# Hybrid decoder block in float32: raw weight blocks in two rings, block sums in a tile of their own, and later squares in the output units

## The chip, the cores and the metric

The kernel runs on one core of one Trainium2 chip. The metric is the device time of one execution in microseconds (us). Before the change three executions took 2388.03, 2392.00 and 2387.68 us, median 2388.03 us; lower is better. A run of this kernel can be told from "no change" at about 0.2%.

## The reference, cut to what matters

One sequence of 256 tokens and 4096 channels in float32 goes through one block. Everything that costs time is matrix products of the 256 x 4096 activations with large weights that are read once:

```
h     = rmsnorm(x, norm_w)
proj  = h @ w_in                     # 4096 x 20480, split in u_p z_p u_c b_c c_c z_c and two gate logits
y_pool = pool(u_p) @ pool_w * pool_scale * silu(z_p)      # four windows 2, 4, 8, 16
y_conv = b_c * conv3(c_c * u_c) * silu(z_c)
merged = sigmoid(g0) * (y_pool @ w_branch[0]) + sigmoid(g1) * (y_conv @ w_branch[1])
out    = rmsnorm(x + merged @ w_out, final_norm_w)
```

`w_in` is 335 MB, `w_branch` 67 MB, `w_out` 67 MB. The results have float32 accuracy.

## The kernel before, in words

**Products.** A float32 number is written as a high part, rounded to the type that TensorE reads fast (`fp32r`), and a low part, the difference. A product is three matmuls: high x high, high x low, low x high. The work is cut into units of 1024 output columns (20 of `w_in`, 8 of `w_branch`, 4 of `w_out`), and a unit into steps (16, or 8 for `w_branch`). A step takes 256 input channels x 1024 columns of weights: four blocks of 128 x 512, in the host's order q0 to q3, 2 KB per partition each. There are two kinds of step. A plain step "P" multiplies the four blocks directly: 8 products, 24 matmuls of 128 x 128 by 128 x 512. A step "S" is one level of a Strassen-like scheme: 7 products, 21 matmuls. It needs the blocks q0, q1, q2 as they are, the corner w = q3 + q2 (the addition is made by an accumulating DMA), and three sums: w - q1, q0 - (w - q1) and q2 - (w - q1). The activations' side of either kind stands ready in SBUF. A unit's order of steps is a text, such as `TEN = "PSPSSPSSPSSPSSPS"` for the gate units or `NINE = "PSPSPSPSSPSPSSPS"` for the second and third output unit. In the last S of a unit ("closing") the order of the seven products is another one. An S runs M2 (block q0), N3 (q1), M1 (q2), N5 (w), N6, N7, N4 (the sums), a closing one M2, N3, N4, M1, N7, N5, N6, three matmuls each. The units in order, with their texts (B and M are small steps of the pooling branch):

```
cz0 16 x P | cb0 NINE_A | cu0 NINE | cc0 NINE_A | cz1 SIX5 | cb1 TEN | cu1 NINE | cc1 NINE_A
pz0 SIX5 | pu0 NINE_P | pz1 HOST | pu1 NINE_P | g0_0 HOST | six gate units TEN | g1_0 SEVEN3
b0_0 B0 | b1_0 B1_FIRST | then three times: b0 B0_MORE, b1 B1 | o0 SIX5 | o1 NINE | o2 NINE | o3 OUT3
SIX5 PPPPPSPSPSPSPSPS   SEVEN3 PPPSPSPSPSPSPSPS   NINE PSPSPSPSSPSPSSPS   NINE_A PSPSSPSPSSPSPSPS
NINE_P PSPSSPSPSSPSSPSP   TEN PSPSSPSSPSSPSSPS   HOST PPBPPMMPSSPSSPSSPSS   OUT3 PSPSPSPSPSPSSPPP
B0 PPPPSPSP   B0_MORE PPPPSSPS   B1_FIRST PPSPSPSP   B1 PSPSPSPP
```

**Preparing a step.** SyncE's queue loads the blocks into a raw slot (`load`, L77): one transfer of 1 MB for P; for S one of 256 KB for q3, one of 768 KB for q0 to q2, and then GpSimd's queue issues the accumulating transfer of q2 onto q3 (`gather`, L89). There are NRAW = 5 raw slots of 8 KB per partition; a slot is loaded again when the step in it is wholly prepared (`prepared`). ScalarE writes the high parts (`highs`, L59) and VectorE the low parts and the sums (`lows` and `sub`, L62). They go to a ring of 26 cells of 2 KB. Cells are given out in order round the ring; a group of cells can be taken when the products that read their former contents have been written into TensorE's program, and on the chip when these have run. A P takes 4 + 4 cells. An S takes 3 + 3 + 4 + 4 cells: high parts of q0 to q2, their low parts, then high and low parts of two blocks twice (`outer`: w - q1 and w; `inner`: the other two sums). The sums overwrite the raw slot.

**Order.** All engines run one hand-written order. While TensorE's matmuls of a step are written down, `pump` writes as much of the preparation of the following steps as the ring and the raw slots allow. Each engine runs its own instructions strictly in that order. Work at the end of a unit (its epilogue) is a list in `queue`: after every 6 matmuls (a tick) one entry is taken off; `gap(n)` is n empty entries. `combine` and `corner_sums` add the unit's separate sums (tile `J`) at the unit's end.

**Output units.** After the output unit c < 3 the epilogue adds the J sums into `E` with two accumulating transfers on GpSimd's queue, adds the rows of x into E with two more (`row`), loads the norm weights with ScalarE's queue (`start`), squares and sums the rows of E on ScalarE (`square`), multiplies E by the weights on VectorE and stores E to `o_d`. The last unit loads these back into raw slots (`unpark`), and the rest of x into another one (`rest`).

Of the kernel before, what the change touches and what calls it, by code (L numbers as in the profile page):

```python
# [27 lines left out]
NRAW = 5  # L28
# [23 lines left out]
def hybrid_block(ctx: ExitStack, tc: tile.TileContext, x, xc, prm, rows_in, w_in, pool_w, w_branch, w_out, out):  # L52
# [56 lines left out]
    raw = sb("raw", [P, NRAW, 2 * NU])  # L109
# [145 lines left out]
    class Step:  # L255
        def __init__(self, unit, kind, src=None, op=None, **kw):
            self.unit, self.kind, self.src, self.op = unit, kind, src, op
            self.__dict__.update(kw)
            self.raw = None
            self.prepared = self.halved = False  # L260
            self.pre, self.mid = [], []

        def first(self):
# [3 lines left out]
            def rounded(cells):  # L267
                self.q = self.raw.rearrange("p (i c) -> p i c", i=4)
                self.cells = cells
                if self in steps[:2]:  # L270
                    for i in range(4):
                        if self is steps[0] and i == 0:
                            copy(ring[:, cells[0]], self.q[:, 0])
                        else:
                            highs(cells[i:i + 1], self.q[:, i:i + 1])
                elif self.halved:
                    for i in (0, 2):
                        highs(cells[i:i + 2], self.q[:, i:i + 2])
                else:
                    highs(cells, self.q[:, 0:len(cells)])  # L280

            return [(3 if self.kind == "S" else 4, None, rounded)]

        def rest(self):
            if self.kind == "P":
                def rests(to):
                    self.lows = to
                    if self in steps[:2]:
                        for i in range(4):
                            if self is steps[0] and i % 2 == 0:  # L290
                                x_low(0, 1 - i // 2)
                            lows(to[i:i + 1], self.cells[i:i + 1], self.q[:, i:i + 1])
                    elif self.halved:
                        for i in (0, 2):
                            lows(to[i:i + 2], self.cells[i:i + 2], self.q[:, i:i + 2])
                    else:
                        lows(to, self.cells, self.q)

                return [(4, None, rests)] + self.mid
            if self.kind == "S":  # L300
                def whole(to):
                    self.lows = to
                    c, q = self.cells, self.q
                    lows(to[1:2], c[1:2], q[:, 1:2])
                    lows([to[0], to[2]], [c[0], c[2]], q[:, 0:3:2])

                def outer(cells):
                    q = self.q
                    self.outer = cells
# [966 lines left out]
```

## Time and profile before

| what | value |
|---|---|
| three executions | 2387.68, 2388.03, 2392.00 us |
| the profiled execution's own time | 2385.66 us |
| its span, first to last instruction | 2383.9 us (1.8 us lie around it) |
| TensorE busy | 2346.6 us, 98% of the span, 10424 matmuls and transposes |
| VectorE busy | 2138.2 us, 90% |
| ScalarE busy | 1488.3 us, 62% |
| GpSimd busy | 287.0 us, 12% |
| mean granted TensorE clock | 0.995 |
| DMA | 627.7 MB, 263 GB/s mean |

PE is TensorE's matmuls, PEld its weight loads, DVE is VectorE, ACT is ScalarE, POOL is GpSimd, SP is SyncE; a name with q (SPq, POOLq) is the engine's queue of DMA issues. "raw<-in_w_in_dram" is a load of input weights into the raw tile. A timeline row starts with the start and the length in us; "x3" means three like instructions merged; in brackets stands how long the engine was idle before it and what ended that. Because matmuls overlap, the row's length holds the drain of the last one.

### The profile page before, as it was taken

The numbers are of one execution on the slowest core, as the hardware profiler recorded it, in microseconds if no ns is written. First come the engines' busy times: TensorE is split into PE (matmuls) and PEld (weight loads), VectorE is DVE, ScalarE is ACT, GpSimd is POOL, SyncE is SP. The second block draws the span as 40 slices with busy tenths as digits, with TensorE's granted clock in tenths as the row PEclk, the third lists the DMA queues.
The fourth block names the chain that finished last, engine by engine and source line by source line (L and its number), as shares of the span: only waits on it lengthen the run. The fifth ranks groups of instructions, "written<-read, shape, count | busy, mean of one in ns | idle before, by whom it ended". The sixth has DMA issues, their size and how long they took to land.

```text
span 2383.9 us, 28821 instructions
## 1 busy us (share of the span) xinstructions
PE 2346.6 (98%) x10424; PEld 1938.5 (81%) x10424; DVE 2138.2 (90%) x2208; ACT 1488.3 (62%) x1565; POOL 287.0 (12%) x342
## 2 busy tenths in 40 slices
PE   9999999999999999999999999999999999999997
PEld 7888888888888888888888888888878887887785
DVE  8799988999979979979999999988998888998887
ACT  6665655756656656656766666665756656556564
POOL 0001100111001201201111111110000100011110
PEclk9999999999999999999999999999999999999998
DMA  9789876988868768868999999999978888887996
GB/s 385 242 254 282 251 239 213 282 258 252 262 221 247 265 197 253 262 199 253 283 284 282 284 303 285 283 281 298 272 226 282 252 281 281 255 256 237 288 271 230
DMA packets 167711, 627.70 MB, mean 263 GB/s; under 512 B 17424, under 2 KB 25872, under 8 KB 135568
## 3 DMA queue, kind: packets, MB, share of 16 engines
q1 hardware_dynamic: 101792, 485.40, 56.9%
q0 software_dynamic: 48128, 98.59, 23.3%
q10 hardware_dynamic: 17648, 41.87, 5.0%
q8 instruction: 81, 1.33, 0.2%
q14 instruction: 62, 0.51, 0.1%
HBM read 579.66 MB, written 25.17 MB: 254 GB/s over the span
## 4 chain that ended last, share of the span: by engine, by line
PE 89%; DMA 4%; DVE 3%; issue 2%; ACT 1%; POOL 0%; SPq 0%; DVEq 0%; ACTq 0%; POOLq 0%
PE sums L1054 64%; PE shared L1054 23%; DVE ring L62 2%; DMA raw<-in_w_out_dram 1%; PE shared L696 1%; DMA E<-in_x_dram 1%; DMA raw<-in_w_branch_dram 1%; PE shared L482 1%; ACT ring L59 1%; DMA E<-J 1%; DMA raw<-in_w_in_dram 1%; DMA raw<-in_x_dram 0%; DVE E L62 0%; DVE raw L62 0%; POOL E L89 0%
## 5 line engine op out<-in xcount | busy, mean ns | idle before, releaser
L59 ACT ACTIVATE ring<-raw 128x1024 fp32r<-128x1024 f32 (+3 forms) x1089 | 1226.1, 1171 | 748.5 <-DVE raw L62 555.2
L1054 PE MATMUL sums<-ring,arena 128*128 128x512 f32 x7011 | 1642.5, 390 | 13.5 <-DVE ring L62 11.1
L62 DVE TENSOR_TENSOR ring<-raw,ring 128x1024 fp32r<-128x1024 f32 (+2 forms) x1338 | 1467.2, 1141 | 147.8 <-ACT ring L59 73.8
L1054 PEld LDWEIGHTS sums<-ring,arena 128*128 128x128 f32 x7011 | 1313.5, 188 | 290.4 <-DVE ring L62 15.5
L1054 PE MATMUL shared<-ring,arena 128*128 128x512 f32 x2241 | 545.8, 391 | 7.6 <-ACT ring L59 5.5
L1054 PEld LDWEIGHTS shared<-ring,arena 128*128 128x128 f32 x2241 | 422.3, 189 | 98.0 <-ACT ring L59 6.3
L62 DVE TENSOR_TENSOR raw<-raw 128x512 f32<-128x512 f32 (+1 forms) x444 | 424.4, 956 | 10.0 <-DMA raw<-in_w_out_dram 2.3
L89 POOL DMA_DIRECT2D raw<-in_w_in_dram x168 | 145.5, 866 | 1362.9 <-DMA raw<-in_w_in_dram 572.1
L62 DVE TENSOR_TENSOR J<-J 128x512 f32<-128x512 f32 (+1 forms) x90 | 78.2, 869 | 14.7 <-ACT J L59 12.5
L1054 PE MATMUL sums<-ring,last_pair 128*128 128x512 f32 x306 | 76.2, 389 | 0.0
L59 ACT ACTIVATE J<-shared 128x512 f32<-128x512 f32 x128 | 69.9, 601 | 4.2 <-PE shared L482 2.9
L1054 PEld LDWEIGHTS sums<-ring,last_pair 128*128 128x128 f32 x306 | 57.4, 188 | 11.9
L59 ACT ACTIVATE E<-sums 128x512 f32<-128x512 f32 x76 | 41.8, 598 | 28.4 <-PE sums L1054 27.6
L89 POOL DMA_DIRECT2D raw<-in_w_out_dram x31 | 28.0, 904 | 258.5 <-DMA raw<-in_w_out_dram 85.5
L89 POOL DMA_DIRECT2D raw<-in_w_branch_dram x23 | 20.0, 869 | 302.4 <-DMA raw<-in_w_branch_dram 142.2
L1054 PE MATMUL shared<-ring,last_pair 128*128 128x512 f32 x216 | 51.9, 389 | 0.0
L1054 PE MATMUL shared<-ring,side 128*128 128x512 f32 x207 | 50.7, 389 | 0.0
L1054 PEld LDWEIGHTS shared<-ring,last_pair 128*128 128x128 f32 x216 | 40.6, 188 | 8.4
L1054 PEld LDWEIGHTS shared<-ring,side 128*128 128x128 f32 x207 | 38.9, 188 | 8.1
L89 POOL DMA_DIRECT2D E<-J x28 | 38.9, 1469 | 13.4 <-ACT ring L59 13.4
L62 DVE TENSOR_TENSOR E<-E,Y 128x2048 f32<-128x2048 f32 x9 | 20.6, 2287 | 7.2 <-ACT Y L59 7.1
L59 ACT ACTIVATE E<-E 128x1024 f32<-128x1024 f32 x16 | 16.7, 1048 | 11.6 <-DMA E<-in_x_dram 11.6
(120 smaller groups left out, 594.7 us busy)
## 6 DMA issues: line engine op xcount, KB each, us to landing
raw<-in_w_in_dram SPq DMA_DIRECT2D x150, 1024.0 KB, 7.2
raw<-in_w_in_dram SPq DMA_DIRECT2D x168, 768.0 KB, 6.8
raw<-in_w_in_dram SPq DMA_DIRECT2D x176, 256.0 KB, 5.1
raw<-in_w_in_dram POOLq DMA_DIRECT2D x168, 256.0 KB, 6.7
raw<-in_w_branch_dram SPq DMA_DIRECT2D x41, 1024.0 KB, 7.5
raw<-in_w_out_dram SPq DMA_DIRECT2D x33, 1024.0 KB, 6.9
raw<-in_w_out_dram SPq DMA_DIRECT2D x31, 768.0 KB, 7.1
raw<-in_w_branch_dram SPq DMA_DIRECT2D x23, 768.0 KB, 6.9
```

What stands on the lines that cost most here:

```text
L59: return pin(nc.scalar.activation(dst, src, func, **kw))
L62: return pin(nc.vector.tensor_tensor(out=dst, in0=a, in1=b, op=op))
L89: return pin(nc.gpsimd.dma_start(dst, src, accum_op=ALU.add))
L482: pin(nc.tensor.transpose(shared(j)[:, i * T + t * P:i * T + (t + 1) * P], src[:, t, c:c + P], ident))
L696: pin(nc.tensor.matmul(o, a, b, start=(k, i) == (0, 0), stop=(k, i) == (3, 2)))
L1054: pin(nc.tensor.matmul(ps, lhs, rhs, start=n == 0, stop=n == u.total[b] - 1))
```

## The change

The raw tile becomes two rings: four places of 6 KB per partition for q0 to q2, and five places of 2 KB for the fourth block ("corner": q3, or w in an S). Both kinds of step load 768 KB and 256 KB apart, so a P has two transfers in place of one. A corner place is loaded again when the step's `summed` is set, which for an S is before its last part; a 6 KB place when the step is prepared. The sums of an S go to a tile of their own, `parts`, of 6 KB; the raw blocks are not overwritten, and w is used as it stands in its place. An S takes 4 + 4 + 6 cells: four high parts; then w - q1 into `parts`, the low part of w, the two other sums; then the high parts of the sums, the low parts of q0 to q2 and the low parts of the sums. A P makes its high and its low parts in runs of three blocks and one, where it made four at once, or two and two after an S. SBUF in use is the same, 40 KB per partition for raw and sums. In the output units the two rows come 3 ticks later, the squares 2 ticks more behind them, and all that follows is as much later. In the last unit `rest` uses J, and the three parked blocks lie across the four 6 KB places.

```diff
-NRAW = 5
+NRAW = 4
+NSUM = 5
-    raw = sb("raw", [P, NRAW, 2 * NU])
+    raw = sb("raw", [P, 3 * NRAW + NSUM, NH])
+    parts = sb("parts", [P, 3, NH])
...
             def rounded(cells):
-                self.q = self.raw.rearrange("p (i c) -> p i c", i=4)
...
-                elif self.halved:
-                    for i in (0, 2):
-                        highs(cells[i:i + 2], self.q[:, i:i + 2])
+                elif self.kind == "S":
+                    highs(cells[3:4], self.corner)
+                    highs(cells[0:3], self.raw)
                 else:
-                    highs(cells, self.q[:, 0:len(cells)])
-            return [(3 if self.kind == "S" else 4, None, rounded)]
+                    highs(cells[0:3], self.raw)
+                    highs(cells[3:4], self.corner)
+            return [(4, None, rounded)]
+        def block(self, i):
+            return self.raw[:, i:i + 1] if i < 3 else self.corner
+        def rests(self, to):
+            self.lows = to
...
+            else:
+                lows(to[0:3], self.cells[0:3], self.raw)
+                lows(to[3:4], self.cells[3:4], self.corner)
+            self.summed = True
...
             if self.kind == "S":
-                def whole(to):
-                    self.lows = to
-                    c, q = self.cells, self.q
-                    lows(to[1:2], c[1:2], q[:, 1:2])
-                    lows([to[0], to[2]], [c[0], c[2]], q[:, 0:3:2])
-                def outer(cells):
-                    q = self.q
-                    self.outer = cells
-                    sub(q[:, 1], q[:, 3], q[:, 1])
-                    sub(q[:, 0:3:2], q[:, 0:3:2], q[:, 1:2].to_broadcast([P, 2, NH]))
-                    highs(cells[0:2], q[:, 1:4:2])
-                    lows(cells[2:4], cells[0:2], q[:, 1:4:2])
-                def inner(cells):
-                    q = self.q
-                    self.inner = cells
-                    highs(cells[0:2], q[:, 0:3:2])
-                    lows(cells[2:4], cells[0:2], q[:, 0:3:2])
-                return [(3, None, whole)] + self.mid + [(4, None, outer), (4, None, inner)]
+                def added(to):
+                    q, w, d = self.raw, self.corner, self.cells
+                    self.lows = to
+                    sub(parts[:, 0], w[:, 0], q[:, 1])
+                    lows(to[3:4], d[3:4], w)
+                    sub(parts[:, 1:3], q[:, 0:3:2], parts[:, 0:1].to_broadcast([P, 2, NH]))
+                    self.summed = True
+                def split(cells):
+                    self.sum_cells, self.sum_lows = cells[0:3], cells[3:6]
+                    highs(cells[0:1], parts[:, 0:1])
+                    highs(cells[1:3], parts[:, 1:3])
+                    lows(self.lows[0:3], self.cells[0:3], self.raw)
+                    lows(cells[3:6], cells[0:3], parts)
+                return [(4, None, added)] + self.mid + [(6, None, split)]
...
-                         "N5": (Q5, formed(3), ("F", 0, 1)),
+                         "N5": (Q5, plain(3), ("F", 0, 1)),
...
-            return gap(3) + [lambda: row(0), None, lambda: row(1)] + gap(3) + [start] + gap(9) + [
+            return gap(6) + [lambda: row(0), None, lambda: row(1)] + gap(3) + [start] + gap(11) + [
                 lambda: square(0), None, lambda: square(1),
...
+    def issue_corner(s):
+        i = s.load_index
+        c = 3 * NRAW + i % NSUM
+        r = raw[:, c]
+        load(r, s.src[:, 3 * NH:])
+        if s.kind == "S":
+            gather(r, s.src[:, 2 * NH:3 * NH])
+        s.corner = raw[:, c:c + 1]
     def issue_load(s):
-        r = raw[:, i % NRAW]
+        r = raw[:, 3 * (i % NRAW):3 * (i % NRAW) + 3]
...
-        elif s.kind == "S":
-            load(r[:, 3 * NH:], s.src[:, 3 * NH:])
-            load(r[:, 0:3 * NH], s.src[:, 0:3 * NH])
-            gather(r[:, 3 * NH:], s.src[:, 2 * NH:3 * NH])
         else:
-            load(r, s.src)
+            load(r.rearrange("p a c -> p (a c)"), s.src[:, 0:3 * NH])
...
     def pump():
+            nc_ = state["corners"]
+            ahead = EARLY if nc_ < 16 else NSUM
+            if 2 <= nc_ < len(loaded) and (nc_ < ahead or loaded[nc_ - ahead].summed):
+                issue_corner(loaded[nc_])
+                state["corners"] += 1
+                moved = True
...
-    def slot(i):
-        return raw[:, (len(loaded) + i) % NRAW].rearrange("p (t n) -> p t n", t=2)
     def unpark(c):
-        parked[c] = slot(c + 1)
+        parked[c] = raw[:, 4 * c:4 * c + 4].rearrange("p (t n) c -> p t (n c)", t=2)
...
-            rest = slot(0)
+            rest = J.rearrange("p (t n) c -> p t (n c)", t=2)
```

50 lines of the change are left out of this document (21 added, 29 removed).

## The prediction

> **What bounds the kernel now.** I read the windows by stage first, to see where TensorE (PE) is not full. Columns: stretch, its length, then busy time (instructions) of PE, PEld, DVE, ACT, POOL, then granted clock, DMA share, GB/s.
>
> ```profile
> 100.00:1700.00 1600.00, 1599.69 (x7135) 1325.94 (x7134) 1460.07 (x1482) 1025.74 (x1054) 215.08 (x259) 1.00 0.86 260
> 1182.00:1583.00 401.00, 401.00 (x1771) 332.16 (x1770) 381.84 (x383) 272.04 (x274) 66.52 (x74) 1.00 0.96 288
> 1700.00:2108.20 408.20, 401.27 (x1793) 330.31 (x1792) 365.09 (x361) 248.45 (x271) 32.59 (x35) 1.00 0.83 261
> 2108.20:2197.30 89.10, 83.76 (x359) 68.08 (x358) 75.98 (x79) 51.12 (x54) 12.09 (x13) 0.96 0.85 257
> 2197.30:2282.60 85.30, 81.83 (x359) 66.87 (x358) 75.63 (x75) 51.10 (x55) 12.10 (x13) 1.00 0.92 270
> 2282.60:2352.40 69.80, 67.74 (x292) 55.56 (x292) 58.48 (x57) 39.97 (x42) 8.66 (x9) 0.98 0.84 253
> ```
>
> From 100 to 1700 us PE never stops, so nothing can be won there; but VectorE (DVE) is busy 381.84 of 401 us in the gate units (95%), so something can be lost. The three output units o1 to o3 are what stands open: PE idles 5.34, 3.47 and 2.06 us in them (length less busy), 10.9 in all. The branch stage idles 6.9.
>
> The chain of waits (start, length, what) gives the units' starts and PE's pace:
>
> ```profile
> 1192.45 6.80 PE sums L1054 x30
> ...
> 2105.47 2.73 PE shared L1054 x12
> 2108.21 6.13 PE sums L1054 x27
> ...
> 2171.47 7.48 PE sums L1054 x33
> ...
> 2197.31 6.80 PE sums L1054 x30
> ...
> 2229.43 8.25 DMA E<-in_x_dram
> ...
> 2282.59 6.13 PE sums L1054 x27
> ```
>
> A closing S ends with 12 "shared" matmuls, so o1 starts at 2108.21; likewise o2 at 2197.31, o3 at 2282.59 and a gate unit at 1192.45. The pace is 7.48 / 33 = 0.2267 us a matmul: a P lasts 5.44 us, an S 4.76, a tick 1.36. At that pace the 359, 359 and 292 matmuls above need 81.4, 81.4 and 66.2 us, so the three units lose 7.7, 3.9 and 3.6 = 15.2 us: the 10.9 idle and 4.3 in slower matmuls. The timeline shows by what:
>
> ```profile
> 2127.27 0.90 POOL L89 DMA_DIRECT2D raw<-in_w_out_dram  x1 [11.66 <-DVE ring L62]
> ...
> 2142.54 0.86 POOL L89 DMA_DIRECT2D E<-in_x_dram  x1 [11.22 <-DMA E<-J]
> 2149.05 1.06 ACT L59 ACTIVATE Y<-E 128x1024 f32<-128x1024 f32 x1 [7.45 <-DMA E<-in_x_dram]
> 2153.36 1.06 ACT L59 ACTIVATE Y<-E 128x1024 f32<-128x1024 f32 x1 [3.17 <-DMA E<-in_x_dram]
> 2155.49 1.22 DVE L62 TENSOR_TENSOR ring<-raw,ring 128x1024 fp32r<-128x1024 f32 x1 [7.75 <-ACT ring L59]
> 2155.51 0.79 PE L1054 MATMUL shared<-ring,arena 128*128 128x512 f32 x1 [4.46 <-ACT ring L59]
> ...
> 2236.53 1.06 ACT L59 ACTIVATE Y<-E 128x1024 f32<-128x1024 f32 x1 [5.83 <-DMA E<-in_x_dram]
> ...
> 2320.05 1.06 ACT L59 ACTIVATE Y<-E 128x1024 f32<-128x1024 f32 x1 [3.54 <-DMA E<-in_x_dram]
> 2325.87 1.06 ACT L59 ACTIVATE Y<-E 128x1024 f32<-128x1024 f32 x1 [4.67 <-DMA E<-in_x_dram]
> 2331.13 2.05 PE L1054 MATMUL sums<-ring,arena 128*128 128x512 f32 x5 [2.06 <-DVE ring L62]
> 2332.98 3.90 PE L1054 MATMUL shared<-ring,arena 128*128 128x512 f32 x12
> ```
>
> ScalarE's square of E waits for the rows of x, every high part is queued behind it, DVE waits for these, and PE stops. This happens in all three units.
>
> **Part 1, the later squares.** Moved are, per unit, two row transfers (POOL), the load of the norm weights (ACT queue), two squares (ACT), one product (DVE) and the store (ACT queue). Counting list entries, the first square moves from tick 25 to 30: from 150 matmuls after the unit's start (34.0 us) to 180 (40.8 us); the second to 192 (43.5 us). Check with o1: 2108.21 + 34.0 = 2142.2, and ACT had come to the square at 2149.05 - 7.45 = 2141.6. New times in o1: 2149.0 and 2151.7, against rows landed at 2149.05 and 2153.36: 1.6 us of waiting left of 10.6. In o2 (2238.1 and 2240.8; landed by 2236.53 and, from the chain, 2229.43 + 8.25 = 2237.7) and o3 (2323.4 and 2326.1, landed by 2320.05 and 2325.87) nothing is left.
>
> That holds if the rows land no later. Their entries come at ticks 12 and 14 (72 and 84 matmuls, 16.3 and 19.0 us after the start), but POOL stands in its raw gather until 2127.27 (19.1 us after) anyway. The new order puts the raw gather of o1's step 10 between the two rows: its corner place comes free in step 5's `added`, written at about 81 matmuls (2126.6), and for 16 us after that J's transfer holds the second row in any case. DVE's product (2.3 us) now comes at 198 matmuls, among single S steps.
>
> Of the idle 10.9 I leave 1.0 for o1's rest. Of the 4.3 in slow matmuls I take 3: they follow the stops, as the last row shows (12 matmuls in 3.90 us with 0.2 of drain, against 2.72, after 2.06 us of standing). [...] **Term: -10 - 3 = -13 us** (bounds -16, all 15.2 and more, and 0, the stall only moved).
>
> **Part 2, the S step.** Durations of the parts (group, count | busy, mean ns | idle):
>
> ```profile
> L62 DVE TENSOR_TENSOR ring<-raw,ring 128x1024 fp32r<-128x1024 f32 x980 | 1170.0, 1222 | 89.3 <-PE sums L1054 48.9 <-ACT ring L59 35.6 <-ACT Y L59 1.0
> L62 DVE TENSOR_TENSOR raw<-raw 128x1024 f32<-128x1024 f32 x222 | 272.1, 1226 | 7.7
> L62 DVE TENSOR_TENSOR ring<-raw,ring 128x512 fp32r<-128x512 f32 x306 | 203.6, 686 | 38.5 <-ACT ring L59 22.2 <-PE sums L1054 8.0 <-ACT E L59 3.4
> L62 DVE TENSOR_TENSOR ring<-raw,ring 128x2048 fp32r<-128x2048 f32 x52 | 118.3, 2286 | 20.0 <-ACT ring L59 16.0 <-PE shared L1054 3.0 <-ACT sa L59 0.8
> L59 ACT ACTIVATE ring<-raw 128x1536 fp32r<-128x1536 f32 x201 | 297.3, 1479 | 23.2 <-PE sums L1054 16.4 <-ACT ring L59 4.6 <-issue 2.1
> ```
>
> Busy over count (overlap out): 512 elements 0.67 us, 1024 1.19, sums of 1024 1.23, 2048 2.28; 1536 on DVE isn't there, and between its neighbours it is 1.74 (bounds 1.19 and 2.28). DVE per S before: 0.67 + 1.19 + 0.69 + 1.23 + 2 x 1.19 = 6.2 us; after: 0.69 + 0.67 + 1.23 + 2 x 1.74 = 6.1. ACT has one short instruction more per S, and a P that was made whole costs 0.1 to 0.2 us more on each engine. All that lies behind PE, which is full: **0**.
>
> Not hidden is the order. Before, DVE made the low parts of q0 to q2 first, which PE's first products need; now they come after the sums and after the low part of w. That one waits for the ring: counting cells back by 26, in "P S S" the low part of w of the second S takes the cell that the P's last product frees, so it can't start before that P ends. From then 0.67 + 1.23 + 1.74 = 3.64 us pass until PE's M2 can start, and PE wants it 4.76 us (one S) after the P's end: **1.1 us to spare**. Before, in the same place, those low parts took cells that the P's 12th matmul frees, 2.72 us before the P's end, and were the first 1.86 us (0.67 + 1.19) of DVE's work: 5.6 us to spare. There are 60 such pairs by the units' texts. If DVE keeps to time they cost 0.
>
> At a unit's end the additions of J push in. 19 times a closing S is followed by "PS". There, relative to the unit's start: w's low part waits for the closing S's N5 (18 of 21 matmuls, -0.68), done at 0; two sums 1.2; J's additions 3.9; low parts 5.6; PE wants them at 5.44. The timeline of the gate unit that starts at 1192.45 shows J's work now:
>
> ```profile
> 1193.21 1.55 ACT L59 ACTIVATE J<-shared 128x512 f32<-128x512 f32 x3
> 1194.80 2.68 DVE L62 TENSOR_TENSOR J<-J 128x512 f32<-128x512 f32 x3 [0.23 <-ACT J L59]
> ```
>
> They give J's 2.68 us. The copies end 2.3 us after the start because high parts of the next S's sums stand ahead of them on ACT; in the new order those come behind, so I let J start at 1.2. So 0.2 us of stop, 19 times: **+4 us** (bounds 0, and 25 if J still ends at 1197.48, 5.0 after the start: low parts at 6.8, 1.3 late, 19 times).
>
> In the branch stage DVE is behind PE already, and a late S there starts after 0.69 + 0.67 + 1.23 + 1.74 = 4.3 us of DVE work where 0.67 + 1.19 were enough, but has less work left under it. I take 0.5 us (half a 1024 pass) for four or so stops of that stage, **+2 us** (bounds -2 and +5).
>
> **Part 3, the transfers.** The first place to look is the start, where load and preparation stand on the path:
>
> ```profile
> 14.78 1.93 ACT ring L59
> 16.73 2.30 DVE ring L62
> 19.08 83.01 PE sums L1054 x365
> ```
>
> This P is made whole; in runs of three and one the first low part needs 1.48 + 1.74 in place of 1.93 + 2.30, **-1 us** (bounds -1 and +1, if the corner loaded first delays the rest).
>
> Afterwards each P has one transfer more. The gate units (1182 to 1583 us) have the most DMA traffic; their queues (packets, MB, share of 16 engines' time) and landing times, and then what SP's queue waits for (us, times, longest):
>
> ```profile
> q1 hardware_dynamic: 18585, 83.89, 57.4%
> q0 software_dynamic: 11936, 25.96, 35.3%
> ...
> raw<-in_w_in_dram SPq DMA_DIRECT2D x31, 1024.0 KB, 7.9
> raw<-in_w_in_dram SPq DMA_DIRECT2D x49, 256.0 KB, 6.7
> raw<-in_w_in_dram POOLq DMA_DIRECT2D x49, 256.0 KB, 7.1
> ```
>
> ```profile
> SPq L77 <- DVE ring L62: 340.8, 109, 6.7
> ```
>
> Four places of 6 KB in place of five give a load three steps, 15 us, to land where it had four, 20 us; it takes 8. The corner with its gather (6.7 + 7.1 = 13.8) keeps five places. So **0**, covered by these 7 us; if a load came later than that, the high parts of its step would be late next. In the tail the rest of x goes to J, which no unit uses any more, and the third parked block waits for the last step's low parts; the last 72 matmuls (16 us) cover its load, **0**, and without them it would cost one landing, 8 us.
>
> **Sum:** -13 + 4 + 2 - 1 = -8 us on 2385.66 (the profiled execution: span 2383.9 + 1.8 around it), 2377.7. The median 2388.03 lies 2.4 higher, so 2380.
>
> **Rivals.** *The preparation order costs more than the squares win (slower).* Place: the second S of a pair; point: DVE late by over 1.1 us at w's low part. For it: DVE busy 95%. Against: the ring wait itself shows that DVE arrives early in a steady run. Price: 0.25 us at each of 60 pairs and 0.6 at 19 boundaries, 15 + 11 = 26 in place of 4: 2402. *The stall moves along:* rows land later by what the squares do, because more raw gathers stand ahead on POOL. Part 1 is 0: 2393. *DMA binds in the gate units:* the 31 P add 31 x 128 = 3968 packets. A 2 KB packet of q0's costs 35.3% x 16 x 401 / 11936 = 190 ns; less 2 KB at q1's mean 44 ns/KB it adds 102 ns: 25 us of 401 per engine, 0.96 + 0.06, so 2% too much, +9 us: 2389. Against: SP waits 340.8 of 401 us for free places, so loads don't queue. [...] In the rows 256 KB lands 1.2 us sooner than 1 MB: a small load pays nearly the whole delay, but whether it costs throughput no row here shows. *All cancels or nothing shows:* 2388.
>
> **How the numbers follow.** Forecast as summed, its own range 2370 to 2383: 0.60. Order too dear: 0.15. Stall only moved: 0.08. DMA bound or cancelled: 0.17. About 0.2% (4.8 us) can be told from none. Faster 0.60, same 0.17, slower 0.23. Range 2368 (all 15.2 + 1 + 2 + 2 won) to 2400 (order's price nearly whole).
>
> **What would show it.** Right: squares start within 2 us of ACT being free, o1 to o3 last near 82, 82 and 67 us, PE stays at 1600 between 100 and 1700 but for stops of tenths of a us at unit starts. Wrong: PE idle of several us between 100 and 1700 ended by DVE ring or ACT ring, above all at an S after an S; or row transfers that land later.

## The result and the profile after

The changed kernel takes 2363.11 us in the median (2362.81 to 2363.51, four executions), the kernel before 2387.86 us beside it (2386.31 to 2392.00). The ratio is 0.9894 (95% interval 0.9877 to 0.9911): 24.75 us faster, where 8 were forecast, and below the low end of the range. The profiled execution took 2362.81 us with a span of 2361.1 us; against the 2383.9 us of before that is 22.8 us, and the stages below add up to it.

The windows of the changed kernel, with the columns of before (stretch, length, busy time of PE, PEld, DVE, ACT, POOL, clock, DMA share, GB/s); the last three are o1, o2 and o3 without its end:

```profile
100.00:1700.00 1600.00, 1599.94 (x7125) 1323.08 (x7125) 1419.43 (x1380) 1042.98 (x1267) 210.80 (x260) 1.00 0.87 260
1182.00:1583.00 401.00, 401.00 (x1767) 330.89 (x1766) 369.05 (x345) 275.90 (x330) 66.53 (x74) 1.00 0.96 287
1700.00:2103.80 403.80, 401.80 (x1800) 331.69 (x1799) 361.08 (x367) 256.44 (x328) 32.63 (x35) 1.00 0.85 267
2103.80:2185.00 81.20, 81.20 (x359) 66.97 (x358) 74.18 (x72) 52.49 (x66) 12.07 (x13) 1.00 0.97 288
2185.00:2266.20 81.20, 81.20 (x358) 66.92 (x357) 72.79 (x68) 52.00 (x65) 12.10 (x13) 1.00 0.96 284
2266.20:2330.00 63.80, 63.80 (x282) 52.54 (x281) 57.40 (x51) 40.33 (x49) 8.60 (x9) 1.00 0.90 270
```

TensorE no longer stops for several us in the output units: o1 lasts 81.2 us instead of 89.1, o2 81.2 instead of 85.3, and the granted clock in o1 is 1.00 instead of 0.96. The branch stage idles 2.0 us instead of 6.9.

The chain of waits of the changed kernel (start, length, what) shows where units begin and where the end comes from:

```profile
1193.17 7.04 PE sums L1061 x30
...
2103.81 7.00 PE sums L1061 x30
...
2184.97 7.04 PE sums L1061 x30
...
2266.15 7.04 PE sums L1061 x30
...
2330.14 9.83 DMA J<-in_x_dram
...
2340.05 2.30 DVE E L63
```

Thirty matmuls at the start of a unit last 7.04 us, where before they lasted 6.80 (the row at 1192.45 us): 0.24 us lost at a unit's start, at 15 of the 18 such starts that the chain lists. The windows count these short stops as busy; they show in the number of matmuls, 7125 in place of 7135 between 100 and 1700 us. At the end the addition still waits for the rest of x, as before:

```profile
2351.21 11.37 DMA raw<-in_x_dram
...
2362.67 2.30 DVE E L62
```

(the kernel before).

GpSimd's and ScalarE's part of the timeline in o1 (start, length, idle time before in brackets):

```profile
2119.26 1.55 POOL L90 DMA_DIRECT2D E<-J  x1
...
2129.41 0.86 POOL L90 DMA_DIRECT2D E<-in_x_dram  x1 [6.45 <-DMA E<-J]
...
2145.35 1.04 ACT L60 ACTIVATE Y<-E 128x1024 f32<-128x1024 f32 x1
...
2149.28 1.04 ACT L60 ACTIVATE Y<-E 128x1024 f32<-128x1024 f32 x1
```

The squares start at once when ScalarE comes to them. The second row of x leaves 25.6 us after the unit's start (2129.41 - 2103.81). Before, it left 34.3 us after it, though its list entry was three ticks earlier: then it waited 11.22 us for J's transfer, now 6.45. J's transfer itself also left sooner, 15.5 us after the unit's start in place of 19.7; before, it left at

```profile
2127.87 1.55 POOL L89 DMA_DIRECT2D E<-J  x1
```

So the rows did not only meet later squares; they came sooner, about half of it because J left sooner and half because it landed sooner. The landing times of these transfers say the same. First the kernel before (queue, count, size, median us from issue to landing; the J row between 1700 and 2105 us):

```profile
E<-J POOLq DMA_DIRECT2D x6, 512.0 KB, 18.1
E<-in_x_dram POOLq DMA_DIRECT2D x6, 512.0 KB, 14.7
```

and the waits that follow from them there, VectorE's and ScalarE's (us in total, times, longest):

```profile
DVE Y L62 <- DMA E<-J: 7.3, 2, 4.4
...
ACT Y L59 <- DMA E<-in_x_dram: 24.7, 5, 7.4
```

In the changed kernel the waits have no row of these two kinds any more, and the landings are:

```profile
E<-J POOLq DMA_DIRECT2D x6, 512.0 KB, 11.6
E<-in_x_dram POOLq DMA_DIRECT2D x6, 512.0 KB, 13.3
```

J's transfers in the branch stage land 11.6 us after their issue in the median instead of 18.1. Nothing in the prediction had this.

The unit starts, read from each kernel's chain, give four stages in us; g1_0 begins with an unbroken run of 78 "sums" matmuls that every chain holds. The lower rows are the experiments below.

| kernel | start to g1_0 | g1_0 to o1 | o1 and o2 | o3 to the end |
|---|---|---|---|---|
| before | 1593.7 | 514.6 | 174.4 | 101.3 |
| changed | 1595.4 | 508.4 | 162.3 | 95.0 |
| before, later squares | 1593.8 | 517.9 | 161.8 | 97.0 |
| before, P loaded in two | 1594.5 | 512.4 | 170.8 | 95.2 |
| before, 2 KB packets | 1594.2 | 510.9 | 165.0 | 95.4 |
| before, 2 KB packets and later squares | 1593.6 | 510.8 | 161.8 | 93.7 |
| changed, old gaps | 1595.9 | 508.4 | 168.6 | 94.9 |
| rings, old order, old gaps | 1593.0 | 512.6 | 170.0 | 99.3 |
| changed, low parts earlier and x earlier | 1592.9 | 507.2 | 161.8 | 93.4 |
| the same with 2 KB packets | 1593.3 | 507.2 | 161.8 | 93.4 |

o1 and o2 hold 714 matmuls (NINE: 7 x 24 + 9 x 21 = 357 each), 161.8 us at 0.2267 us: at this pace, which is that of fp32r operands (no run has these products in another type), that column can go no lower. The gain of 22.8 us is 12.0 in o1 and o2, 6.4 from o3 on, 6.1 in the branch stage, less 1.7 up to g1_0.

### The profile page after: what moved, and what is told of

Read it like the earlier page. It is cut to its first block, busy times and chain, and to the rows that moved or that the text cites. A ratio compares the mean times of both kernels' runs of the same rounds, so it can differ in the third digit from the quotient of the medians.

```text
span 2361.1 us, 29582 instructions
## 1 busy us (share of the span) xinstructions
PE 2343.1 (99%) x10424; PEld 1935.2 (82%) x10424; DVE 2089.1 (88%) x2108; ACT 1517.3 (64%) x1879; POOL 282.5 (12%) x342
## 3 DMA queue, kind: packets, MB, share of 16 engines
q1 hardware_dynamic: 134624, 485.42, 58.8%
## 4 chain that ended last, share of the span: by engine, by line
PE 97%; DVE 2%; DMA 1%; ACT 0%; issue 0%; SPq 0%; DVEq 0%; ACTq 0%
PE sums L1061 69%; PE shared L1061 25%; PE shared L690 1%; PE shared L476 1%; DVE ring L63 1%; DMA J<-in_x_dram 0%; ACT ring L60 0%; DVE E L63 0%; DMA raw<-in_w_in_dram 0%; DVE parts L63 0%; DVE arena L63 0%; PE shared L666 0%; ACT sa L60 0%; DVE Y L63 0%; DVE raw L1223 0%
## 5 line engine op out<-in xcount | busy, mean ns | idle before, releaser
L63 DVE TENSOR_TENSOR ring<-raw,ring 128x512 fp32r<-128x512 f32 (+2 forms) x982 | 1088.6, 1134 | 175.5 <-PE shared L1061 68.4
L60 ACT ACTIVATE ring<-raw 128x512 fp32r<-128x512 f32 (+1 forms) x945 | 901.7, 1013 | 140.3 <-PE sums L1061 116.0
L60 ACT ACTIVATE ring<-parts 128x512 fp32r<-128x512 f32 (+1 forms) x458 | 375.5, 831 | 517.9 <-DVE parts L63 466.3
L63 DVE TENSOR_TENSOR ring<-parts,ring 128x1536 fp32r<-128x1536 f32 (+2 forms) x256 | 390.9, 1538 | 14.2 <-PE sums L1061 7.8
L63 DVE TENSOR_TENSOR parts<-raw,parts 128x1024 f32<-128x1024 f32 x222 | 270.8, 1220 | 0.0
L63 DVE TENSOR_TENSOR parts<-raw 128x512 f32<-128x512 f32 x222 | 152.4, 687 | 2.2 <-DVE ring L63 0.4
L1061 PEld LDWEIGHTS sums<-ring,last_pair 128*128 128x128 f32 x306 | 57.3, 188 | 12.7 <-DVE ring L63 0.9
```

What stands on the lines that cost most here:

```text
L60: return pin(nc.scalar.activation(dst, src, func, **kw))
L63: return pin(nc.vector.tensor_tensor(out=dst, in0=a, in1=b, op=op))
L1061: pin(nc.tensor.matmul(ps, lhs, rhs, start=n == 0, stop=n == u.total[b] - 1))
```

## The experiments

Ratios are to the kernel before on the same chip. Its own median there lay between 2383.4 and 2387.9 us, and single executions of it spread over some 10 us; those of the changed kernel over less than 1 us. So gains over the kernel before are given as ratios, and two versions of the changed kernel are set side by side by their times. The stage table has one execution of each kernel.

### Each half alone

*Later squares in the kernel before.*

```
-            return gap(3) + [lambda: row(0), None, lambda: row(1)] + gap(3) + [start] + gap(9) + [
+            return gap(6) + [lambda: row(0), None, lambda: row(1)] + gap(3) + [start] + gap(11) + [
```

> The kernel before with only the later rows and squares. Theory 'squares' (the output units were won by the squares alone): ScalarE's wait for the rows falls from 24.7 us to under 4, o1, o2, o3 last near 82, 82 and 67 us to the last unit's tail, and the time falls by 13 to 18 us, to 2370 to 2375. Rival 'order' (it was the new order of preparing that carried the output units over the same wait): less than 6 us, over 2381.

Measured: 2369.68 us, ratio 0.9946 (0.9928 to 0.9964), about -13 us by the ratio (15 by the medians). Its window over the output units is full:

```profile
2105.00:2330.00 225.00, 225.00 (x993) 186.04 (x992) 208.14 (x206) 142.08 (x151) 33.62 (x36) 1.00 0.93 282
```

(before: 215.26 busy of 225). The two squares of o1 waited 0.42 us together. The edit acts in the output units alone: there 16.9 us in the stage table (12.6 + 4.3), the end included. The branch stage, in which the code is the same, came out 3.3 us longer in this execution, which shows how much that stage wanders by itself.

*The opposite: the changed kernel with the gaps of before* (the same line turned round).

> The changed kernel with the rows and squares put back to their old ticks. Theory 'squares': 12 to 17 us slower than the changed kernel, 2375 to 2380, with TensorE stopping in o1 to o3 again. Rival 'order': within 4 us of the changed kernel, 2360 to 2367, although ScalarE waits for the rows again.

Measured: 2369.13 us, ratio 0.9943 (0.9923 to 0.9962), between the two theories. The rings and the new S order are worth as much alone as the squares alone, and 12.2 of their 16.1 us in the profile lie from o1 on (5.8 in o1 and o2, 6.4 behind them), in the stages that the squares repair too. The later squares give only 6 us on top of them. The two halves overlap; neither is a cost on the whole.

### What in the rings helps

*The kernel before, a P loaded as 256 and 768 KB into the same five slots.*

```
-            load(r, s.src)
+            load(r[:, 3 * NH:], s.src[:, 3 * NH:])
+            load(r[:, 0:3 * NH], s.src[:, 0:3 * NH])
```

> The kernel before, each plain step loaded by 256 KB and 768 KB in place of 1 MB, into the same five slots. Theory 'packets' (J's accumulating transfers were slow because they share the DMA engines with rows of 8 KB): between 1700 and 2108 us E<-J lands in 13 us or less (18.1 before), VectorE's 11.7 us of waiting for it in the branch stage go to under 3, the time falls by 3 to 6 us. Rival 'in flight' (five slots of 8 KB let too many bytes stand ahead): E<-J stays at 16 us and more there, the time within 2 us of before.

Measured: 2374.16 us, ratio 0.9959 (0.9944 to 0.9973). One load in two pieces, with nothing else changed, makes the kernel 0.4% faster, more than the 3 to 6 us expected, though J lands after 14.3 us and not within 13:

```profile
E<-J POOLq DMA_DIRECT2D x6, 512.0 KB, 14.3
...
E<-in_x_dram POOLq DMA_DIRECT2D x6, 512.0 KB, 13.7
```

*Four slots of 8 KB in the kernel before*, so that less is under way at a time (`rest` goes to J, as in the changed kernel).

```
-NRAW = 5
+NRAW = 4
```

> The kernel before with four slots of 8 KB in place of five (the rest of x goes to J). Theory 'in flight': E<-J lands in 13 us or less between 1700 and 2108 us and the time falls by 3 to 6 us. Rival 'packets': E<-J stays at 16 us and more, and the time is the same or up to 6 us longer, since loads have one step less to land.

Measured: 2395.05 us, ratio 1.0054 (1.0035 to 1.0073), 10 us slower by the medians, more than the 6 of the rival theory. J lands after 19.4 us, no sooner, and VectorE now waits for weights:

```profile
DVE Y L62 <- DMA E<-J: 17.1, 3, 8.9
DVE raw L62 <- DMA raw<-in_w_in_dram: 16.4, 6, 3.4
DVE raw L62 <- DMA raw<-in_w_out_dram: 15.4, 5, 5.5
```

That fewer loads under way let J's transfers through is refuted. (x lands after 13.1 us here, but it does so after 13.5 with the later squares alone, too: its landing depends on more than the loads.)

*The changed kernel's two rings with the old S order, sums in place, and the old gaps.*

```
+                def whole(to):
...
+                    lows(to[1:2], c[1:2], q[:, 1:2])
+                    lows([to[0], to[2]], [c[0], c[2]], q[:, 0:3:2])
+                def outer(cells):
...
+                    sub(q[:, 1], w[:, 0], q[:, 1])
+                    sub(q[:, 0:3:2], q[:, 0:3:2], q[:, 1:2].to_broadcast([P, 2, NH]))
...
+                return [(3, None, whole)] + self.mid + [(4, None, outer), (4, None, inner)]
```

> The two rings of the changed kernel with the old order of preparing an S (3, 3, 4, 4 cells, sums over the raw blocks) and the old ticks for the squares. VectorE and ScalarE have one short instruction more per S than the old kernel, since w lies in another place. To be set against the changed kernel with old ticks (0.57% below the kernel before). Theory 'order': 8 us and more above that one. Rival 'rings': within 4 us of it. Unit starts take 6.80 us for their first 30 matmuls again, not 7.04, by both.

Measured: 2375.30 us, ratio 0.9958 (0.9942 to 0.9975): as much as the split load alone. The rings as such add nothing to it. With the new order on the same rings it was 0.9943, so the order and the tile of sums are worth some 0.15% there (6.2 us by the times, between the two theories). By the table 4.2 us of that lie in the branch stage (508.4 against 512.6); there TensorE stands idle 2.0 us of 405 in place of 5.8, and over the whole run VectorE waits for ScalarE's ring cells 25 times (43.3 us) in place of 141 (92.8 us).

*The other way round: new S order and tile of sums, but four slots of 8 KB and loads of 1 MB* (old gaps; w is `q[:, 3]` of the slot).

```
-NRAW = 5
+NRAW = 4
...
+    parts = sb("parts", [P, 3, NH])
...
```

> Four slots of 8 KB loaded whole, old ticks for the squares, but the changed kernel's order of preparing an S and its tile of sums. To be set against four slots with the old order (0.54% above the kernel before). Theory 'order' (beside the squares it is the new order that wins, since VectorE has fewer and longer passes and waits less for ScalarE): 8 to 14 us under that one, 0.0 to 0.2% below to above the kernel before. Rival 'rings' (it is the split loading into two rings): within 4 us of it, still 0.4% and more above the kernel before.

Measured: 2393.03 us, ratio 1.0036 (1.0021 to 1.0050), between the two theories. Against four slots with the old order (1.0054) the new order gives little; like those it waits for late weights (9.9 us of `parts` for `w_out`). Without the rings it is of little use here; whether for the corner place, which they free earlier, or for the loads in two transfers was not separated.

### Two transfers or shorter packets

The split load differs from the old one in two things: a P comes in two transfers, and its packets are 6 and 2 KB long instead of 8 (134624 packets in its q1 in place of 101792, 485.4 MB in both). Two kernels, both otherwise the kernel before, tell these apart.

*All weight loads in transfers of 256 KB.*

```
+        order = range(4) if i < 2 or s.kind != "S" else (3, 0, 1, 2)
+        for k in order:
+            load(r[:, k * NH:(k + 1) * NH], s.src[:, k * NH:(k + 1) * NH])
...
```

> The kernel before, with each load of raw weights made in transfers of 256 KB: four for a P (where before had one of 1 MB) and four for an S (where before had 256 and 768 KB), so that every packet of these loads is 2 KB long. Five slots of 8 KB, order of work and gaps as before. Theory 'packets' (long packets of the weight loads hold up the other queues' small transfers, E<-J above all): more than the split into 256 + 768 KB alone gave, so 2366 to 2374 us (2374.2 there, 2384 to 2388 before), and E<-J lands within 14 us of its issue in the median between 1700 and 2105 us (18.1 before, 14.3 with the split). Theory 'first part' (the split wins because the highs of a P can start on a part of it): the wait is on the whole place, so no more than the split gave, 2373 to 2378 us. Rival: four issues per step cost more on the queue than the packets give, 2385 us or more.

*A P in one transfer of 1 MB as before, but the slot's four blocks apart in SBUF, so that each packet is 2 KB.*

```
-    raw = sb("raw", [P, NRAW, 2 * NU])
+    raw = sb("raw", [P, 4, NRAW, NH])
...
-        r = raw[:, i % NRAW]
+        r = raw[:, :, i % NRAW]
...
-            load(r, s.src)
+            load(r, s.src.rearrange("p (k c) -> p k c", k=4))
```

> The kernel before, with the slots laid so that a slot's four blocks of 2 KB are not neighbours in SBUF: a P is still one transfer of 1 MB and an S still 256 + 768 KB, but every packet is 2 KB long. The last unit's rest of x goes to J, the three parked blocks lie across the raw tile. Theory 'packets': as the loads in quarters, 2366 to 2376 us, and E<-J within 14 us in the median between 1700 and 2105 us. Theory 'two transfers' (what counts is that a P arrives in two pieces): within 3 us of before, 2383 to 2389 us, E<-J at 17 to 19 us. Rival: 2 KB packets are dearer to move, then slower than before, above 2390 us.

Measured: 2370.49 us, ratio 0.9930 (0.9917 to 0.9942), and 2366.59 us, ratio 0.9918 (0.9905 to 0.9932). In the first the slots lie as before; in the second the number of transfers is as before, and it gains at least as much. What they share is the packet of 2 KB: it is the packets. J's median landing time follows their length in the kernels of this section and the split load. From the queues of the kernel before (packets, MB, share of 16 engines' time over the span):

```profile
q1 hardware_dynamic: 101792, 485.40, 56.9%
```

and of the kernel with one transfer in 2 KB packets, with the landing of J (1700 to 2105 us) and of x:

```profile
q1 hardware_dynamic: 246176, 485.40, 59.6%
...
E<-J POOLq DMA_DIRECT2D x6, 512.0 KB, 11.2
...
E<-in_x_dram POOLq DMA_DIRECT2D x6, 512.0 KB, 11.6
```

For J in the branch stage it is 18.1 us with packets of 8 KB, 14.3 with 6 and 2, 11.2 with 2 (10.7 in four transfers); for x 14.7 (13.5 with the later squares), 13.7, 11.6 and 10.6. TensorE's waits in the branch stage fall from 6.8 us before to 3.8 in the kernel with one transfer in 2 KB packets. J's and x's transfers go out on GpSimd's queue, the weight loads on SyncE's (POOLq and SPq in the rows). What delays them beside longer packets no run shows. Other transfers gain little. Over the whole run, first before, then with one transfer in 2 KB packets:

```profile
raw<-in_w_in_dram SPq DMA_DIRECT2D x150, 1024.0 KB, 7.2
raw<-in_w_in_dram POOLq DMA_DIRECT2D x168, 256.0 KB, 6.7
...
E<-J POOLq DMA_DIRECT2D x28, 512.0 KB, 12.0
```

```profile
raw<-in_w_in_dram SPq DMA_DIRECT2D x150, 1024.0 KB, 7.8
raw<-in_w_in_dram POOLq DMA_DIRECT2D x168, 256.0 KB, 6.6
...
E<-J POOLq DMA_DIRECT2D x28, 512.0 KB, 10.9
```

The raw gathers of `w_in` on the same queue land hardly sooner, and the 1 MB loads themselves land 0.6 us later. That packets act is shown; why they act on J and x in these stages most is not.

Four loads of 256 KB came out 0.12% behind one of 1 MB in equal packets, but the intervals overlap: that the number of transfers costs anything by itself is not shown.

### Are packets and squares the whole?

*The kernel before with the 2 KB packets and the later squares*, no ring, no new order (the two diffs above together).

> The kernel before with two edits: its weight loads in packets of 2 KB at unchanged transfers (2366.6 us by itself, -19.6) and the later rows and squares in the output units (2369.7 us by itself, about -15). No rings, no tile of sums, the old order of an S. Theory 'packets and squares are the whole': what the changed kernel gains (2363.1 us) comes from the shorter packets of its loads and from the squares, the new order of an S gives nothing of its own: 2358 to 2364 us, the two overlapping by 10 to 15 us in the output units. Theory 'the new order has a part of its own': 2364 to 2367 us, above the changed kernel, with some wait of TensorE in the branch stage that the changed kernel has not. Rival: the later squares collide with the better timed rows, no gain over the packets alone, 2366.6 or more.

Measured: 2363.54 us, ratio 0.9913 (0.9899 to 0.9928). The time of the changed kernel is reached without its rings, its tile or its order, though by ratio (0.9894) the changed kernel lies a little lower, within the intervals. It is reached in another way: up to g1_0 this kernel has no stops at unit starts, and in the branch stage it is 2.4 us slower (510.8 against 508.4). The changed kernel's own packets are of 6 and 2 KB; these with the later squares alone were not run.

*The changed kernel with two repairs (`both`, below) and 2 KB packets in its 768 KB loads too.*

```
-        r = raw[:, 3 * (i % NRAW):3 * (i % NRAW) + 3]
+        r = raw[:, i % NRAW:3 * NRAW:NRAW]
```

> The changed kernel with the two edits of the run before (2357.4 us) and its 6 KB places laid as three blocks of 2 KB apart from each other, so that the 768 KB loads too have packets of 2 KB. Theory 'packets act through the J transfers': VectorE and ScalarE had no wait for E left in the changed kernel, so no more than 2 us either way: 2355.5 to 2358.5 us, though E<-J lands sooner than its 11.6 us between 1700 and 2105 us. Theory 'packets act on every transfer that TensorE waits for': the branch stage's last stops (403.5 of 405 us busy) go too, 2353 to 2355.5 us. Rival: more packets on a DMA share of 96% in the gate units delay the weights there, 2359 us or more.

Measured: 2357.29 us, ratio 0.9889 (0.9872 to 0.9905), against 2357.41 without it. x lands after 11.1 us in place of 12.7, and it is worth nothing, since no square waits for x there. For J this is hardly a test: with the two repairs it lands after 7.7 us already, and after 7.5 with the shorter packets. That the packets gain through the waits for J and x fits this. The 2 KB packets in the old kernel say it more plainly: there VectorE's 7.3 us of waiting for J in the branch stage went to none, and the squares' 24.7 us of waiting for x to 13.7.

Set beside the kernel of the run before, on the same chip and with the same packets and squares, this one is 6.2 us faster (2357.02 to 2357.44 against 2361.61 to 2363.63). In the profile it is 4.2 us, and 3.6 of them lie in the branch stage. So rings and new order do have a part of their own; in the changed kernel the stops at unit starts hide it.

### The order's own cost, and the end

*The changed kernel with the low parts of q0 to q2 at the end of `added`*, ahead of J's additions at a unit's start:

```
                     sub(parts[:, 1:3], q[:, 0:3:2], parts[:, 0:1].to_broadcast([P, 2, NH]))
+                    lows(to[0:3], d[0:3], q)
...
-                    lows(self.lows[0:3], self.cells[0:3], self.raw)
```

> The changed kernel with the low parts of q0 to q2 made at the end of the first part of an S (behind the sums, ahead of J's additions) and not in its last. If J's additions are what makes the first S of a unit late, the first 30 matmuls of units after a closing S take 6.80 us again in place of 7.04, and 19 x 0.24 = 4.5 us go: 2357 to 2360. If they are late for another reason, 2362 to 2364 as the changed kernel.

Measured: 2358.70 us, ratio 0.9888 (0.9870 to 0.9907), 4.4 us below the changed kernel's median. The two unit starts that its chain shows between 1100 and 1200 us last 6.80 us again, as do all 19 in the chain of `both`, which has the same edit.

*The same low parts at the very front of `added`, ahead of the sums.*

```
                     self.lows = to
+                    lows(to[0:3], d[0:3], q)
                     sub(parts[:, 0], w[:, 0], q[:, 1])
...
-                    lows(self.lows[0:3], self.cells[0:3], self.raw)
```

> The changed kernel with the low parts of q0 to q2 of an S written first in its part `added`, ahead of the three sums. Theory of the boundary term (at a unit's start TensorE waits for the low parts of the first S because VectorE makes the three sums and J's additions first): the low parts are earlier still, so the stops of 0.24 us at 19 unit starts go as in the kernel with the lows at the end of that part, 2357 to 2360 us. Rival: ScalarE, which makes the high parts of the sums, now gets its input 5 us later, and the matmuls N6, N7 and N4 wait in every S or the two engines alternate less well: slower than the changed kernel, 2365 to 2385 us.

Measured: 2458.37 us, ratio 1.0306 (1.0291 to 1.0320), 95 us slower than the changed kernel, far beyond the rival's 2365 to 2385. The waits of VectorE and TensorE (us in total, times, longest) and the window of the long middle:

```profile
DVE ring L63 <- ACT ring L60: 269.9, 254, 4.5
...
PE shared L1061 <- DVE ring L63: 48.1, 41, 2.4
PE sums L1061 <- DVE ring L63: 11.0, 21, 1.3
```

```profile
100.00:1600.00 1500.00, 1452.12 (x6358) 0.99 0.83 244
```

VectorE waits for ScalarE 254 times (in the changed kernel 25 times, 43.4 us). VectorE's low parts come first, ScalarE waits for the sums, and then VectorE waits for ScalarE's high parts of them. The timeline of one S:

```profile
402.68 1.75 DVE L63 TENSOR_TENSOR ring<-raw,ring 128x1536 fp32r<-128x1536 f32 x1
...
405.12 0.63 ACT L60 ACTIVATE ring<-parts 128x512 fp32r<-128x512 f32 x1 [3.67 <-DVE parts L63]
...
407.95 1.76 DVE L63 TENSOR_TENSOR ring<-parts,ring 128x1536 fp32r<-128x1536 f32 x1 [1.19 <-ACT ring L60]
```

The 1.75 us of low parts are the work under which these high parts are made in the changed kernel; moved ahead, VectorE, whose 369 of 401 us in the gate units leave it little room, stands idle 1.19 us in this S, and TensorE stops: 59 us of waiting in the two rows above. Most of the rest is in matmuls and short stops counted as busy, 2381.1 us for the same 10424 matmuls that take 2343.1 in the changed kernel.

*The rest of x loaded at the start of the last unit's lead[-4], not at the closing of its first bank.*

```
         if st is lead[-4]:
             flush()
             last.before()
+            rest = J.rearrange("p (t n) c -> p t (n c)", t=2)
+            move(rest, xrows[:, :, 3 * NU:])
...
-            rest = J.rearrange("p (t n) c -> p t (n c)", t=2)
-            move(rest, xrows[:, :, 3 * NU:])
```

> The changed kernel with the load of the rest of x some 10 us sooner in the last unit. If the first token half's finishing waits for that load (it landed 0.08 us before the addition that opens the finishing), 1 to 2 us go: 2361 to 2362. If the finishing is held by TensorE's last products alone: 2363, no change.

Measured: 2361.69 us, ratio 0.9901 (0.9885 to 0.9916), -1.4 us. No transfer is left in the end of its chain, which is now TensorE's last matmuls:

```profile
2331.97 17.01 PE sums L1061 x75
```

*Both repairs:*

> The changed kernel with two edits: the low parts of q0 to q2 of an S are written at the end of its part `added` rather than in `split` (2358.7 us by itself, -4.4), and the rest of x is loaded at the last unit's fourth step from the end of its lead rather than at the closing of its first bank (2361.7 us by itself, -1.4). They act at other places (unit starts; the last 20 us), so they should add: 2363.1 - 4.4 - 1.4 = 2357 us (2355.5 to 2358.5). Rival: with TensorE free of stops at unit starts, the tail is bound by something else and the second edit gives nothing: 2358.7.

Measured: 2357.41 us (2357.04 to 2357.68), ratio 0.9879 (0.9866 to 0.9893). They add as expected; this version is faster than both kernels.

## Why the prediction was wrong, point by point

Two steps failed: the transfers, put at 0, and the branch stage, put at +2 us. By stages of the profiled execution, with the boundary term spread over its 19 unit starts at 0.2 us each, forecast and measured (in us, minus is faster) were +1.6 and +1.7 up to g1_0, +2.6 and -6.1 in the branch stage, -12.4 and -18.4 from o1 on. In the branch stage the new order, priced as a cost, gave 4.2 us and the shorter packets, put at nothing, 2.2. From o1 on 3.9 us of the miss are Part 1's size, as the squares alone show, and about 2 lie at the end. The packets by themselves are worth more, but mostly in the stages that the squares repair too. The signs that the prediction named for being right (squares that start at once, full output units, stops of tenths of a us at unit starts) did come, so Parts 1 and 2 hold in their mechanism.

**Part 1, later squares: right in kind, too small.** The three output units were to give 13 us; alone the edit gave 16.9 from o1 to the end. "I leave 1.0 for o1's rest" and "of the 4.3 in slow matmuls I take 3" were both too careful: nothing was left, and o1 and o2 run at the matmul floor of 161.8 us (0.2267 us a matmul). The step that J's transfer holds the second row for 16 us "in any case" held in the kernel with the later squares alone (15.7 us from the issue of J to the row, 10.89 of them waited for J), but not in the changed kernel (10.2, and 6.45). With the long stops gone the clock is 1.00 in every window above, the one with the 2.06 us stop (0.98 before) included. So all of the slow matmuls went with the stops.

**Part 2, the S step: the order was priced well.** The boundary term was 0.2 us x 19 = 4. The chain shows 0.24 us at 15 of 18 unit starts, and taking it away gave 4.4 us. The 1.1 us to spare at an S after an S sufficed: up to g1_0 the kernel loses 1.7 us, and ten such starts (2.4) less what the start of the kernel gives (0.6, below) are 1.8, so nothing is left for the pairs. The rival that the order is too dear did not come; the run with the low parts in front shows what a wrong order costs, though by ScalarE's part of the chain, which the prediction had not counted.

**The start: right, half the size.** -1 us was forecast. The first long run of matmuls begins 0.6 us sooner than at 19.08 us before:

```profile
18.51 83.07 PE sums L1061 x365
```

**The branch stage: a step that failed, wrong sign.** +2 us was taken for a later first product; measured -6.1. VectorE's wait there for J's transfer (7.3 us) had been in the trace of before, but the prediction held it fixed and asked only what the new order adds. The changed kernel's own packets in the old order gave 2.2 us (512.4 in the table, 512.6 with rings), the new order with its tile of sums on the same rings and gaps 4.2 (508.4). So the order, priced here as a cost, gives most of this stage. Each number is of one execution, and the stage wandered by 3.3 us in the run with the later squares; but the kernels with the rings and the new order (low parts in front left aside) lie at 507.2 to 508.4, and all with shorter packets and the old order at 510.7 to 512.6.

**Part 3, the transfers: the other step that failed.** "So 0", covered by 7 us of slack, asked whether the weights come late. It didn't ask how transfers on the other queues land beside the weights' packets (J's in the branch stage after 18.1 us with packets of 8 KB, 11.2 with 2). The split P load, costed at nothing, is worth 10.7 us by itself by the medians (2374.16 against 2384.86; 0.41% by the ratio), most of it from o1 on (9.7 of 11.1 in the profile), where it overlaps with what the squares give. The rival built on this step had the wrong sign: it priced a further packet at 102 ns from the 190 ns of the accumulating queue. By the rows above, 144384 more packets cost 59.6% x 16 x 2365.4 - 56.9% x 16 x 2383.9 = 853 us of engine time, 5.9 ns each by this estimate; the same sum gives 12 ns for the split load and 10 for the four transfers of 256 KB.

**The end: 0 forecast.** From o3's start on 6.4 us were gained. The unit's own stops of before were 3.6; the rest of x was on the chain before (its row starts at 2351.21, 68.6 us after o3's start) and goes out after 64.0 us now, 1.0 sooner than the stops explain, and takes 9.83 us in place of 11.37. So about 2.7 us come from there. The prediction looked only at whether the new place in J costs something.

**How the parts add.** On the kernel before, 2 KB packets gave 0.82%, later squares 0.54%, both together 0.87% (each within 0.2%). Both repair the same stop in the output units: one brings the rows sooner, the other the squares later. A sum of separate terms could not hold there. In the branch stage, which the squares don't touch, terms have room to add.

**What stays open.** With the rings the new order gives some 6 us more (0.9958 to 0.9943, the intervals overlap). In the trace J's transfers land after 10.7 us with it and 13.3 without; whether they are less held up by raw gathers, or meet fewer loads, was not separated. With 2 KB packets and later squares on both sides some 4 to 6 us are left to the rings and the order (with the two repairs), most of it in the branch stage. Why shorter packets bring J and x sooner, and the raw gathers of `w_in` hardly, is open too.

## What to carry to other kernels

When a kernel's small transfers land late beside large loads, look at the packet length of the loads before their number: a destination cut into 2 KB rows cost some 6 ns for each packet added here, by the estimate above, and brought the transfers that engines waited for home 3 to 7 us sooner. Two repairs of one stall didn't add here; cost each against the kernel that has the other. And when the order on one engine is turned, write down which of its work covers the other engine's part: 1.75 us of low parts in the wrong place in every S cost 95 us.

## What the runs showed of the hardware that was not expected

Packet length: the landing of 512 KB on GpSimd's queue went from 14.7 to 11.6 us (x) and from 18.1 to 11.2 us (J, branch stage) as the other queue's packets went from at most 8 KB to 2 KB, at unchanged bytes and nearly unchanged engine time (56.9 to 59.6% of a shorter span). All 28 transfers of J together went only from 12.0 to 10.9 us, and the 1 MB loads took 7.8 us in place of 7.2. Transfers of 256 KB in place of 1 MB did no visible harm to the total (2370.49 us against 2366.59 in equal packets, ratios 0.9930 and 0.9918 with overlapping intervals, 485 MB in q1 in either case).
